# A two-layer hybrid attention trunk: copies and spills leave SP's queue, attention runs a few steps behind its projections

## The chip, the cores and the metric

The kernel runs on one core of a Trainium2 chip. A core has five engines that each run their own instruction stream in order: TensorE (PE) for matmuls, VectorE (DVE), ScalarE (ACT), GpSimd (POOL) and SyncE (SP), which in this kernel only issues DMA transfers. The metric is the device time of one execution in microseconds, lower is better. Matmul operands come from SBUF, results stand in PSUM, and weights, inputs and spilled tensors lie in HBM.

## The reference

Two layers, 512 tokens, width 1024, all float32. Each layer normalises its input, multiplies it by one wide matrix, runs two attention branches of the same input, gates them, projects them and adds the result to the input. Cut to its lines:

```python
h  = rms_norm(x, norm_w)
u  = h @ w_in                         # 1024 x 10240
qa, ka, va, za, qb, kb, vb, zb, ga, gb = split_cols(u)
qa, ka, qb, kb = partial_rope(...)    # first 16 of 64 channels of each head
ya = dilated_mixture(qa, ka, va) * silu(za)            # 16 heads of 64
ob = softmax(q1 k1) v - lam * softmax(q2 k2) v         # 8 heads, v of width 128
yb = rms_norm(ob, subln_w) * (1 - lam_init) * silu(zb)
merged = sigmoid(ga) * (ya @ w_proj_a) + sigmoid(gb) * (yb @ w_proj_b)
x  = x + merged @ w_out
...
return rms_norm(x, final_norm_w)
```

All attention is causal. `dilated_mixture` comes down to one softmax with a fixed additive bias that counts how many of three (window, dilation) patterns hold a pair of positions.

## The kernel before, in words

**Layout.** Activations stand transposed, channels on the 128 partitions and the 512 tokens in the free dimension. Each float32 operand is split into a rounded part and the rest (`split` for weights: `whi` by ACT at L102, `wlo` by DVE at L103), and each product is three matmuls: high by high, high by low, low by high (L264 to L266, L279 to L281).

**Weights.** `stream` lays the weights out as pieces of 512 KB in the order in which they are used. `load_to` issues a piece (`raw`, L96) on SP into a slot of the pool `blk`, `split` turns it into `whi` and `wlo` in a pool of three slots each. `blk` has 32 slots of 4 KB per partition, which nearly every large tile shares.

**Projections.** `proj_S` (gates and values v) works with seven products of sums of weight and activation blocks in place of eight; it has eight pieces, and POOL fetches the ones that are added (`T`, L112). `proj_T` (q/k of one unit, or one z tile) has two pieces and 48 matmuls of 512 columns, `proj_V` (`pa`, the projection of branch A) two pieces and 96 of 256 columns, `proj_W` (`pb` and `out`) four pieces.

**A layer.** First two z tiles, gate 0, v of branch A, gate 1, q/k of unit 0, v of branch B. Gates and v are spilled to HBM by SP (L442, L463). Then come 16 windows, one for each of 16 units: units 0 to 7 are pairs of heads of branch A, units 8 to 15 heads of branch B. Names carry (layer, branch, unit), so (0, 1, 6) is the seventh head of branch B in layer 0. Window w projects q/k of unit w+1, in some windows also a z tile or a quarter of `pa`, and beside them does the scores of unit w (`s_steps`, L477 to L508) and the values of unit w-1 (transposes `t` at L523, `o` at L555 and L613, in branch B also the norm `rms` with POOL's power at L224, `scale` at L636, the turn `ot` at L641, and `yf`, `yb`). `mix` orders the steps of the two units, and `run` spreads them evenly over the projection's steps of that window. After window 15, `pb` (with the values of unit 15 beside it), `out` and the next layer follow.

**q and k.** `ev_qk` takes the projection out of PSUM: DVE shuffle (L408) and product (L410), POOL product `sw` (L411), DVE sum (L412), ACT and DVE split (L418, L419) into `hl`, and then ten DMA copies by `move` (L403) that put the two halves of the partitions where the score matmuls want them: four of 64x512 into `qx`, and for each of two `kx` one of 64x1024 and two of 64x512. Scores of a unit start with the matmul L498 on `kx`.

**What sets the order.** The functions above emit instructions in a program order; then the tile framework's scheduler, with a timeline model of its own, orders each engine's stream. On the chip each stream runs in order, so an instruction that waits holds all behind it, DMA issues on SP's queue included.

Of the kernel before, what the change touches and what calls it, by code (L numbers as in the profile page):

```python
# [9 lines left out]
F32 = mybir.dt.float32  # L10
# [6 lines left out]
P = 128  # L17
# [15 lines left out]
def trunk_kernel(ctx: ExitStack, tc: tile.TileContext, x, xtok, ws, norm_w, subln_w, final_w, lams, negb, rope,  # L33
# [1 line left out]
    nc = tc.nc  # L35

    fix = ctx.enter_context(tc.tile_pool(name="fix", bufs=1))
    blk = ctx.enter_context(tc.tile_pool(name="blk", bufs=32))
    wpool = ctx.enter_context(tc.tile_pool(name="wpool", bufs=3))
    att = ctx.enter_context(tc.tile_pool(name="att", bufs=2))  # L40
    tmp = ctx.enter_context(tc.tile_pool(name="tmp", bufs=10))
# [46 lines left out]
    def load_to(i):  # L88
        while n_load[0] < min(i, len(loads)):
            j = n_load[0]  # L90
            if loads[j][0] == "add":
                n_load[0] += 1
                continue
            raw[j] = f4(f"raw{j}")
            to = raw[j].rearrange("p a t -> p (a t)")
            nc.sync.dma_start(to, ws[j])  # L96
            n_load[0] += 1

# [301 lines left out]
        return st_["h"][k]  # L400

    def move(to, of):
        nc.sync.dma_start(bits(to), bits(of))  # L403

    def ev_qk(key):
        def f(b, ps):
# [30 lines left out]
    def ev_v(layer, br):  # L437
        def f(tb, half, src):
            v = t2(f"v{layer}{br}{tb}{half}") if (tb >= 2 and half == 0) else src
            nc.scalar.activation(v, src, AF.Copy, scale=st_["rcol"][:, tb:tb + 1])  # L440
            to = v_dram[layer, br, 4 * half:4 * half + 4, :, tb].rearrange("u p c -> p u c")
            nc.sync.dma_start(to, v.rearrange("p (u c) -> p u c", u=4))  # L442
        return f

    def load_v(key, store):
# [13 lines left out]
    def ev_gate(layer, which):  # L459
        def f(tb, half, src):  # L460
            g = t2(f"g{layer}{which}{tb}{half}") if (tb >= 2 and half == 0) else src
            nc.scalar.activation(g, src, AF.Sigmoid, scale=st_["rcol"][:, tb:tb + 1])
            nc.sync.dma_start(g_dram[layer, which, tb, :, T * half:T * half + T], g)  # L463
        return f

    def ev_z(key):
# [8 lines left out]


    def s_steps(key, half, br, store):  # L477
        qx, kx = st_["qk"][key][0], st_["qk"][key][1 + half]
        mn = small.tile([P, 4], F32, tag="mn", name=f"mn{key}{half}")
        den = small.tile([P, 4], F32, tag="den", name=f"den{key}{half}")  # L480
        pr = store["p", half] = []
        store["den", half] = den

        def s(i):
            n = (i + 1) * P
            ps = pss.tile([P, T], F32, tag="s", name=f"s{key}{half}{i}")
            q = qx[:, half, i * P:(i + 1) * P]
# [19 lines left out]
            pr.append(p)  # L507
        return [(520, lambda i=i: s(i)) for i in range(4)]  # L508

    def t_steps(key, pr):  # L510
        def t(which):
            ps = pst.tile([P, T], F32, tag="t", name=f"t{key}{which}")
# [12 lines left out]
            nc.vector.tensor_tensor(dst[:, 1], ps[:, :n], bits(dst[:, 0]), OP.subtract)  # L525
        return [(440, lambda w=w: t(w)) for w in range(3)]
# [11 lines left out]
    def a_pair(layer, u):  # L538
# [34 lines left out]
        def scores(half):  # L573
            ss = s_steps(key, half, 0, store)
            if half == 0:
                load_v(key, store)
            else:
                ss = [(0, lambda: split_v(key, store))] + ss
            w, f = ss[-1]
            ss[-1] = (w, lambda: (f(), norm(half)))  # L580
            return ss

        def values(half):
            vv = t_steps((key, half), store["p", half]) + [(1200, lambda: pv(half))]
            return vv + [(0, fin)] if half else vv
        return scores, values

    def b_head(layer, u):
# [49 lines left out]
        def turn():  # L638
# [8 lines left out]
            nc.scalar.activation(y[:, 0], f, AF.Copy)  # L647
            nc.vector.tensor_tensor(y[:, 1], f, bits(y[:, 0]), OP.subtract)
            if u < 6:
                nc.sync.dma_start(yb_dram[layer, u], bits(y))  # L650

        def scores(half):
            ss = s_steps(key, half, 1, store)
            if half == 0:
                load_v(key, store)
            else:
                ss = [(0, lambda: split_v(key, store))] + ss
                w, f = ss[-1]
# [2 lines left out]

        def values(half):
            if half == 0:
                return t_steps((key, 0), store["p", 0]) + [(900, lambda: pv(0)), (900, lambda: pv(1))]
            return [(0, rms), (0, scale), (0, lambda: None), (430, turn)]
        return scores, values

    def back(layer):

        for u in range(6):  # L670
            y = st_["y"][layer, 1, u] = b4(f"yr{layer}{u}")
            nc.sync.dma_start(bits(y), yb_dram[layer, u])
# [27 lines left out]
    def gate(layer, which):  # L700
        return lambda: proj_S((layer, "gate", which), ev_gate(layer, which))

    pres = {}

    def pa(layer, i):

        c = slice(256 * i, 256 * i + 256)

        def pre():
            st_["pg", i] = f4(f"pg{layer}{i}").rearrange("p a (b c) -> p (a b) c", b=2)  # L710
            nc.sync.dma_start(st_["pg", i], g_dram[layer, 0, :, :, c].rearrange("t p c -> p t c"))

        def ev(tb, ps):
            t = st_["pg", i]
            nc.vector.tensor_tensor(t[:, tb], ps[:, :256], t[:, tb], OP.mult)
            if tb == 3:
                nc.sync.dma_start(pa_dram[layer, :, :, c].rearrange("t p c -> p t c"), t)
        pres[i] = pre
        return lambda: proj_V((layer, "pa", i), lambda k: st_["y"][layer, 0, k], ev)

    def turned(name, of):
# [35 lines left out]
    def outp(layer, i):  # L757
# [8 lines left out]

        def ev(tb, ps):
            nc.vector.tensor_tensor(r[tb], ps, r[tb], OP.add)
            nc.sync.dma_start(x1_dram[tb, :, i], r[tb])
            square(layer + 1, tb, i, r[tb])  # L770

        def turn(j):
# [91 lines left out]
    for layer in range(DEPTH):  # L864
# [64 lines left out]
def windows():  # L929
# [108 lines left out]
```

## Time and profile before

| | |
|---|---|
| runs | 1494.71, 1498.1 and 2704.91 us, median 1498.1 |
| profiled execution | 1494.3 us, its span 1492.5 us |
| mean granted TensorE clock | 0.967 of full speed |
| PE busy | 1389.8 us, 93% of the span |
| DVE, ACT, POOL busy | 1011.1 us (68%), 870.9 us (58%), 137.3 us (9%) |
| HBM traffic | 155.53 MB read, 31.46 MB written |

The profile shows one execution. Busy times are sums over a whole engine; PE's share is high everywhere, so what matters is where its idle time and its lower clock lie, and what ended each wait. In layer 0 the windows run from about 200 us to 650 us of the span, in layer 1 from about 950 us to 1400 us. Between and ahead of them lie the long projections.

### The profile page before, as it was taken

What the parts mean: (1) busy time and instruction counts of PE and PEld (TensorE: products, weight loads), DVE (VectorE), ACT (ScalarE), POOL (GpSimd) and SP (SyncE); (2) the same over time, 40 slices, a digit from 0 to 9 for tenths busy, and PEclk for the clock granted to TensorE, in tenths of its full rate; (3) what the DMA queues carried; (4) which work ended last, traced back from release to release, by engine and by line L of the source; (5) the groups of instructions that cost most, each with busy time, mean ns of one, the idle gap of its engine ahead of it and who ended that gap; (6) DMA issues with size and microseconds to landing.
All of it is one profiled execution on the core that took longest, in us unless ns stands there. A gap on an engine that the chain in (4) does not pass through costs nothing.

```text
span 1492.5 us, 19895 instructions
## 1 busy us (share of the span) xinstructions
PE 1389.8 (93%) x6856; PEld 1159.5 (78%) x6856; DVE 1011.1 (68%) x1959; ACT 870.9 (58%) x1655; POOL 137.3 (9%) x127
## 2 busy tenths in 40 slices
PE   7899999999989998889989999999999898997996
PEld 6788887877879787778878888878777786886785
DVE  6765667777777677635576667687777767767454
ACT  7866567776844645532367665668766545546232
POOL 2000001001010011000020000010111110010000
PEclk9999999999999999889999999999999999998998
DMA  9875634454365472962387746444444563729521
GB/s 340 221 192 144 195 103 119 122 169 114 106 163 170 148 207 76 298 258 71 132 203 189 208 100 184 127 113 114 141 131 128 157 186 97 233 78 335 193 71 57
DMA packets 108308, 238.63 MB, mean 160 GB/s; under 512 B 12464, under 2 KB 37168, under 8 KB 108208
## 3 DMA queue, kind: packets, MB, share of 16 engines
q1 hardware_dynamic: 103600, 220.58, 47.6%
q0 software_dynamic: 4608, 16.78, 6.5%
q8 instruction: 54, 0.88, 0.2%
q14 instruction: 46, 0.38, 0.1%
HBM read 155.53 MB, written 31.46 MB: 125 GB/s over the span
## 4 chain that ended last, share of the span: by engine, by line
PE 63%; DVE 10%; issue 9%; DMA 8%; ACT 6%; SPq 2%; POOL 0%; ACTq 0%; DVEq 0%; POOLq 0%
PE pj L264 8%; PE pj L265 8%; PE pj L266 8%; PE X L279 4%; PE X L280 4%; PE X L281 4%; DMA raw<-ws_d 3%; PE pw L279 2%; PE pw L280 2%; PE pw L281 2%; PE Y L281 2%; PE Y L280 2%; PE Y L279 2%; SPq L403 2%; ACT whi L102 1%
## 5 line engine op out<-in xcount | busy, mean ns | idle before, releaser
L103 DVE TENSOR_TENSOR wlo<-raw,whi 128x1024 fp32r<-128x1024 f32 x208 | 257.2, 1236 | 193.9 <-ACT whi L102 192.7
L102 ACT ACTIVATE whi<-raw 128x1024 fp32r<-128x1024 f32 x208 | 219.7, 1057 | 217.4 <-PE pw L281 77.4
L264 PE MATMUL pj<-h,whi 128*128 128x512 f32 x768 | 307.2, 403 | 15.2 <-DVE h L190 9.2
L265 PE MATMUL pj<-h,whi 128*128 128x512 f32 x768 | 304.9, 397 | 0.0
L266 PE MATMUL pj<-h,wlo 128*128 128x512 f32 x768 | 302.3, 395 | 0.0
L264 PEld LDWEIGHTS pj<-h,whi 128*128 128x128 f32 x768 | 145.8, 190 | 49.9 <-issue 9.2
L266 PEld LDWEIGHTS pj<-h,wlo 128*128 128x128 f32 x768 | 146.2, 190 | 29.5
L265 PEld LDWEIGHTS pj<-h,whi 128*128 128x128 f32 x768 | 146.3, 191 | 28.0 <-DVE h L191 0.4
L103 DVE TENSOR_TENSOR wlo<-T,whi 128x1024 fp32r<-128x1024 f32 x48 | 60.8, 1269 | 40.8 <-ACT whi L102 40.7
L102 ACT ACTIVATE whi<-T 128x1024 fp32r<-128x1024 f32 x48 | 50.6, 1055 | 18.3 <-PE Z L281 6.1
L280 PE MATMUL X<-wlo,h 128*128 128x512 f32 x128 | 51.2, 400 | 4.0 <-DVE wlo L103 4.0
L279 PE MATMUL X<-whi,h 128*128 128x512 f32 x128 | 48.2, 402 | 3.9 <-DVE z(1, 0, 0)_6927 L471 3.5
L279 PE MATMUL pw<-whi,mg 128*128 128x512 f32 x128 | 50.9, 400 | 0.0
L281 PE MATMUL X<-whi,h 128*128 128x512 f32 x128 | 50.9, 398 | 0.0
L280 PE MATMUL pw<-wlo,mg 128*128 128x512 f32 x128 | 49.9, 391 | 0.0
L280 PE MATMUL Y<-wlo,S 128*128 128x512 f32 x128 | 49.8, 389 | 0.0
L281 PE MATMUL Y<-whi,S 128*128 128x512 f32 x128 | 49.8, 389 | 0.0
L280 PE MATMUL X<-wlo,S 128*128 128x512 f32 x128 | 49.8, 389 | 0.0
L281 PE MATMUL X<-whi,S 128*128 128x512 f32 x128 | 49.8, 389 | 0.0
L281 PE MATMUL pw<-whi,mg 128*128 128x512 f32 x128 | 47.8, 393 | 0.0
L112 POOL DMA_DIRECT2D T<-ws_d x32 | 27.8, 870 | 200.3 <-ACT T L111 199.0
L279 PE MATMUL Y<-whi,S 128*128 128x512 f32 x128 | 44.9, 390 | 0.9 <-ACT whi L102 0.9
(3827 smaller groups left out, 3341.6 us busy)
## 6 DMA issues: line engine op xcount, KB each, us to landing
raw<-ws_d SPq DMA_DIRECT2D x192, 512.0 KB, 5.7
T<-ws_d POOLq DMA_DIRECT2D x32, 512.0 KB, 6.4
g_dram<-c SPq DMA_DIRECT2D x24, 256.0 KB, 2.2
v_dram<-c SPq DMA_DIRECT2D x24, 256.0 KB, 2.6
yr<-yb_dram SPq DMA_DIRECT2D x12, 512.0 KB, 8.8
pg<-g_dram SPq DMA_DIRECT2D x8, 512.0 KB, 4.3
pa_dram<-pg SPq DMA_DIRECT2D x8, 512.0 KB, 5.0
m<-g_dram SPq DMA_DIRECT2D x16, 256.0 KB, 7.5
```

The costliest lines, as they stand in the source:

```text
L102: nc.scalar.activation(whi[j], src, AF.Copy)
L103: nc.vector.tensor_tensor(wlo[j], src, bits(whi[j]), OP.subtract)
L112: nc.gpsimd.dma_start(out=flat(t), in_=add, accum_op=OP.add)
L264: nc.tensor.matmul(ps, w_h, hb[:, 0], start=(k == 0), stop=False)
L265: nc.tensor.matmul(ps, w_h, hb[:, 1], start=False, stop=False)
L266: nc.tensor.matmul(ps, w_l, hb[:, 0], start=False, stop=(k == 7))
L279: nc.tensor.matmul(ps, hh, w_h, start=first, stop=False, skip_group_check=True)
L280: nc.tensor.matmul(ps, hh, w_l, start=False, stop=False, skip_group_check=True)
L281: nc.tensor.matmul(ps, hl, w_h, start=False, stop=last, skip_group_check=True)
L403: nc.sync.dma_start(bits(to), bits(of))
```

## The change

Five edits. `move`, and the stores of `yb`, `pa` and `x1`, are issued by POOL in place of SP. The spills of gates and v are issued by ACT, which also computes them. SP keeps the loads. The weight pieces of `proj_T`, `proj_V` and `proj_W` get three slots of their own, and `blk` goes from 32 slots to 29; the pieces of `proj_S` stay in `blk`. The z tiles come behind q/k in their windows, and were ahead. And `run` for each window gives way to one `merge` over all 17 windows of a layer: a window's attention steps are placed by accumulated weights of the projection's steps, `LAG` = 6000 weights (about nine steps of `proj_T`) after the window's start and end. The 17th window is the values of the last head over the first 0.7 of `pb`'s first half. The functions `s_steps` and `t_steps` look up their tiles when a step runs, since steps now run later than the lists are made, and `load_v` is a step in the list.

```diff
+LAG = 6000
...
-    blk = ctx.enter_context(tc.tile_pool(name="blk", bufs=32))
+    blk = ctx.enter_context(tc.tile_pool(name="blk", bufs=29))
...
-            raw[j] = f4(f"raw{j}")
-            to = raw[j].rearrange("p a t -> p (a t)")
+            if loads[j][0] == "S":
+                t = f4(f"raw{j}")
+            else:
+                t = wpool.tile([P, 2, T], F32, tag="raw", name=f"raw{j}")
+            raw[j], to = t, flat(t)
             nc.sync.dma_start(to, ws[j])
...
     def move(to, of):
-        nc.sync.dma_start(bits(to), bits(of))
+        nc.gpsimd.dma_start(bits(to), bits(of))
...
-            nc.sync.dma_start(to, v.rearrange("p (u c) -> p u c", u=4))
+            nc.scalar.dma_start(to, v.rearrange("p (u c) -> p u c", u=4))
...
-            nc.sync.dma_start(g_dram[layer, which, tb, :, T * half:T * half + T], g)
+            nc.scalar.dma_start(g_dram[layer, which, tb, :, T * half:T * half + T], g)
...
-                nc.sync.dma_start(yb_dram[layer, u], bits(y))
+                nc.gpsimd.dma_start(yb_dram[layer, u], bits(y))
...
-                nc.sync.dma_start(pa_dram[layer, :, :, c].rearrange("t p c -> p t c"), t)
+                nc.gpsimd.dma_start(pa_dram[layer, :, :, c].rearrange("t p c -> p t c"), t)
...
-            nc.sync.dma_start(x1_dram[tb, :, i], r[tb])
+            nc.gpsimd.dma_start(x1_dram[tb, :, i], r[tb])
...
+    def merge(main, side):
+
+        done, j = 0.0, 0
+        for w, f in main:
+            f()
+            done += w
+            while j < len(side) and side[j][0] <= done:
+                side[j][1]()
+                j += 1
+        for _, f in side[j:]:
+            f()
...
-        for w, names in enumerate(WINDOWS):
-
-            side = []
-            for half in range(2):
-                here = heads[w][0](half)
-                side += mix(here, heads[w - 1][1](half)) if w else here
-            main = chain(*[todo[n[0]](layer, *n[1:]) for n in names])
-            main = [(0, pres[n[1]]) for n in names if n[0] == "pa"] + main
-            run(main + [(0, lambda: back(layer))] if w == 15 else main, side)
+
+        main, side = [], []
+        for w in range(17):
+            names = WINDOWS[w] if w < 16 else []
+            here = [heads[w][0](half) if w < 16 else [] for half in range(2)]
+            there = [heads[w - 1][1](half) if w else [] for half in range(2)]
+            steps = mix(here[0], there[0]) + mix(here[1], there[1])
+            new = [(0, pres_of(layer, n[1])) for n in names if n[0] == "pa"]
+            new += chain(*[todo[n[0]](layer, *n[1:]) for n in names])
+            if w == 15:
+                new.append((0, lambda: back(layer)))
+            if w == 16:
+                b = [pb(layer, i) for i in range(2)]
+                new = b[0][0]()
+            first, length = sum(m[0] for m in main), sum(m[0] for m in new)
+            end = first + length * (0.7 if w == 16 else 1) + LAG * (w < 15)
+            first += LAG * (w < 16)
+            side += [(first + (end - first) * (j + 1) / (len(steps) + 1), f) for j, (_, f) in enumerate(steps)]
+            main += new
+        merge(main, side)
...
-        w[at].insert(0, ("z", s // 4, s % 4))
+        w[at].append(("z", s // 4, s % 4))
```

Lines behind the edits are four to five higher in the changed kernel (`move` L403 is L407, `ot` L641 is L646), and about 17 higher from `merge` on. The scheduler orders each engine anew. SP issues 321 transfers where it issued 733, POOL 348 more than before, ACT 64 more; the matmuls and DVE's instructions are the same in number. Three places show the new order.

**SP around head (0, 1, 6) of layer 0.** `raw` is a weight piece, `vf` the reload of v, `pg` that of a gate. Before:

```order
L403 DMA qx(0, 1, 6)_5351<-hl(0, 1, 6)0_5348 64x512 x4
L96 DMA raw_5384<-ws_d 128x1024
L447 DMA vf(0, 1, 6)_5442<-v_dram 128x512
L650 DMA yb_dram<-yb(0, 1, 4)_5416 128x1024
L403 DMA kx(0, 1, 6)0_5432<-hl(0, 1, 6)1_5429 64x512
L403 DMA kx(0, 1, 6)0_5432<-hl(0, 1, 6)1_5429 64x1024
L403 DMA kx(0, 1, 6)0_5432<-hl(0, 1, 6)1_5429 64x512
L403 DMA kx(0, 1, 6)1_5436<-hl(0, 1, 6)1_5429 64x1024
L403 DMA kx(0, 1, 6)1_5436<-hl(0, 1, 6)1_5429 64x512 x2
L711 DMA pg_5446<-g_dram 128x4x256
L96 DMA raw_5452<-ws_d 128x1024
```

In the change:

```order
L100 DMA raw_5213<-ws_d 128x1024
L100 DMA raw_5270<-ws_d 128x1024
L100 DMA raw_5376<-ws_d 128x1024
L100 DMA raw_5410<-ws_d 128x1024
L451 DMA vf(0, 1, 5)_5204<-v_dram 128x512
L724 DMA pg_5404<-g_dram 128x4x256
L100 DMA raw_5506<-ws_d 128x1024
L100 DMA raw_5563<-ws_d 128x1024
L100 DMA raw_5730<-ws_d 128x1024
L451 DMA vf(0, 1, 6)_5497<-v_dram 128x512
```

The copies into `qx` and `kx` and the store of `yb` stood between the weight pieces; now only loads stand there.

**POOL around head (0, 1, 7).** `sw` is the rotary product of `ev_qk` (0 behind the bracket for q, 1 for k), `rs` the power of a head's norm. Before:

```order
L224 TENSOR_TENSOR rs(0, 1, 3)_4924<-rs(0, 1, 3)_4924,mhalf 128x4
L411 TENSOR_TENSOR sw(0, 1, 6)0_5342<-sw(0, 1, 6)0_5342,st 128x512
L224 TENSOR_TENSOR rs(0, 1, 4)_5251<-rs(0, 1, 4)_5251,mhalf 128x4
L411 TENSOR_TENSOR sw(0, 1, 6)1_5423<-sw(0, 1, 6)1_5423,st 128x512
L411 TENSOR_TENSOR sw(0, 1, 7)0_5505<-sw(0, 1, 7)0_5505,st 128x512
L411 TENSOR_TENSOR sw(0, 1, 7)1_5580<-sw(0, 1, 7)1_5580,st 128x512
L224 TENSOR_TENSOR rs(0, 1, 5)_5559<-rs(0, 1, 5)_5559,mhalf 128x4
L224 TENSOR_TENSOR rs(0, 1, 6)_5859<-rs(0, 1, 6)_5859,mhalf 128x4
L224 TENSOR_TENSOR rs(0, 1, 7)_6081<-rs(0, 1, 7)_6081,mhalf 128x4
```

In the change:

```order
L415 TENSOR_TENSOR sw(0, 1, 7)0_5462<-sw(0, 1, 7)0_5462,st 128x512
L407 DMA qx(0, 1, 7)_5471<-hl(0, 1, 7)0_5468 64x512 x4
L228 TENSOR_TENSOR rs(0, 1, 4)_5315<-rs(0, 1, 4)_5315,mhalf 128x4
L735 DMA pa_dram<-pg_5404 128x4x256
L415 TENSOR_TENSOR sw(0, 1, 7)1_5535<-sw(0, 1, 7)1_5535,st 128x512
L655 DMA yb_dram<-yb(0, 1, 4)_5483 128x1024
L407 DMA kx(0, 1, 7)0_5544<-hl(0, 1, 7)1_5541 64x512
L407 DMA kx(0, 1, 7)0_5544<-hl(0, 1, 7)1_5541 64x1024
L407 DMA kx(0, 1, 7)0_5544<-hl(0, 1, 7)1_5541 64x512
L407 DMA kx(0, 1, 7)1_5548<-hl(0, 1, 7)1_5541 64x1024
L407 DMA kx(0, 1, 7)1_5548<-hl(0, 1, 7)1_5541 64x512 x2
L228 TENSOR_TENSOR rs(0, 1, 5)_5628<-rs(0, 1, 5)_5628,mhalf 128x4
```

Between the two `sw` of a unit there are now the four copies into `qx`, an `rs` and a store; the six copies into `kx` come behind them.

**PE at the turn `ot` of a head of branch B.** `o` are its values, `pj` and `pv` projections, `s` scores, `t` transposes. Before, at head (0, 1, 2):

```order
L613 MATMUL o(0, 1, 2)1_4642<-vt(0, 1, 2)_4364,pt_103 128x256 x2
L265 MATMUL pj_1_4884<-h_7_190,whi_4745 128x512
L266 MATMUL pj_1_4884<-h_7_190,wlo_4746 128x512
L641 MATMUL ot(0, 1, 2)_4774<-ident,of(0, 1, 2)_4615 128x128 x4
L523 MATMUL t((0, 1, 3), 0)0_4826<-ident,p(0, 1, 3)0_4547 128x128
```

In the change, at the same head; the last of its `o` stands 76 rows above `ot`, and 68 of the rows between are `pv` matmuls:

```order
L284 MATMUL pv_3_5070<-wlo_4772,ya(0, 0, 0)_2097 128x256
L285 MATMUL pv_3_5070<-whi_4771,ya(0, 0, 0)_2097 128x256
L283 MATMUL pv_3_5070<-whi_4771,ya(0, 0, 1)_2322 128x256
L284 MATMUL pv_3_5070<-wlo_4772,ya(0, 0, 1)_2322 128x256
L646 MATMUL ot(0, 1, 2)_4841<-ident,of(0, 1, 2)_4679 128x128 x4
L528 MATMUL t((0, 1, 3), 0)0_4876<-ident,p(0, 1, 3)0_4596 128x128
```

In the change, at head (0, 1, 5), whose turn before had 14 rows of `pj` ahead of it and `o` farther up:

```order
L618 MATMUL o(0, 1, 5)1_5660<-vt(0, 1, 5)_5366,pt_103 128x256 x2
L507 MATMUL s(0, 1, 7)01_5851<-kx(0, 1, 7)0_5544,qx(0, 1, 7)_5471 128x256
L508 MATMUL s(0, 1, 7)01_5851<-kx(0, 1, 7)0_5544,qx(0, 1, 7)_5471 128x256
L507 MATMUL s(0, 1, 7)02_5871<-kx(0, 1, 7)0_5544,qx(0, 1, 7)_5471 128x384
L508 MATMUL s(0, 1, 7)02_5871<-kx(0, 1, 7)0_5544,qx(0, 1, 7)_5471 128x384
L646 MATMUL ot(0, 1, 5)_5806<-ident,of(0, 1, 5)_5627 128x128 x4
L528 MATMUL t((0, 1, 6), 0)0_5826<-ident,p(0, 1, 6)0_5524 128x128
```

The turn of (0, 1, 2) moved away from its `o`, that of (0, 1, 5) moved close to it.

## Rows read from the trace of the kernel before

**Rows 1.** The page: busy us of each engine, share of the span, instructions.

```profile
PE 1389.8 (93%) x6856; PEld 1159.5 (78%) x6856; DVE 1011.1 (68%) x1959; ACT 870.9 (58%) x1655; POOL 137.3 (9%) x127
```

**Rows 2.** Windows: stretch, length, busy us by engine, PEclk, DMA share, GB/s.

```profile
75.00:100.00 25.00, 24.90 (x111) 20.28 (x110) 14.98 (x13) 17.55 (x22) 3.45 (x4) 1.00 0.73 165
200.00:650.00 450.00, 414.00 (x2177) 349.12 (x2176) 326.40 (x760) 275.93 (x613) 45.64 (x37) 0.95 0.54 160
625.00:650.00 25.00, 17.55 (x67) 13.19 (x66) 17.35 (x49) 16.23 (x40) 1.01 (x1) 0.63 1.03 398
650.00:950.00 300.00, 295.27 (x1329) 242.55 (x1328) 181.63 (x214) 161.07 (x214) 22.36 (x23) 0.99 0.54 153
950.00:1400.00 450.00, 412.76 (x2179) 348.80 (x2178) 322.41 (x752) 272.24 (x611) 44.35 (x36) 0.95 0.55 163
```

**Rows 3.** PE's waits: who waits, for whom, us in total, times, longest.

```profile
PE ot(1, 1, 2)_11351 L641 <- DVE of(1, 1, 2)_11192 L636: 6.4, 1, 6.4
PE ot(0, 1, 2)_4774 L641 <- DVE of(0, 1, 2)_4615 L636: 6.0, 1, 6.0
PE ot(0, 1, 6)_5971 L641 <- DVE of(0, 1, 6)_5858 L636: 4.2, 1, 4.2
...
PE X L279 <- DVE z(1, 0, 0)_6927 L471: 3.5, 1, 3.5
...
PE ot(0, 1, 4)_5409 L641 <- DVE of(0, 1, 4)_5250 L636: 3.0, 1, 3.0
PE s(0, 0, 6)00_3104 L498 <- DMA kx(0, 0, 6)0_3080<-hl(0, 0, 6)1_3077: 2.8, 1, 2.8
...
PE t((1, 1, 6), 0)0_12377 L523 <- DVE p(1, 1, 6)0_12052 L603: 1.1, 3, 0.6
...
PE s(0, 0, 4)00_2588 L498 <- DMA kx(0, 0, 4)0_2564<-hl(0, 0, 4)1_2561: 1.0, 1, 1.0
```

**Rows 4.** SP's queue: waits of its DMA issues, in the same columns.

```profile
SPq L96 <- DVE wlo L103: 70.2, 18, 17.6
...
SPq L442 <- ACT c L440: 50.6, 23, 9.6
...
SPq L403 <- ACT hl(0, 1, 6)0_5348 L418: 20.1, 1, 20.1
```

**Rows 5.** The chain of waits around 515 us: start, length, what.

```profile
510.50 0.23 PE pj L266
510.73 0.12 PE o(0, 1, 2)0_4608 L613
...
514.02 0.53 ACT hl(0, 1, 4)0_4713 L418
...
514.57 0.47 SPq L403
...
515.73 4.54 DMA raw<-ws_d
...
520.37 1.06 ACT whi L102
...
522.85 1.02 POOL rs(0, 1, 2)_4616 L224
...
524.83 1.13 PE ot(0, 1, 2)_4774 L641 x4
```

**Rows 6.** Line L403: durations min, median, max in ns; landing of its copies.

```profile
L403 SPq DMA_DIRECT2D qx(0, 0, 3)_2162<-hl(0, 0, 3)0_2159 x4: 462/556/603, 262.6 to 264.4; - x4
...
DMA to landing us min/median/max: 2.2/3.3/9.3
```

**Rows 7.** Line L112: POOL's DMA issues, durations min, median, max in ns.

```profile
L112 POOL DMA_DIRECT2D T<-ws_d x32: 837/862/1052, 25.7 to 903.1; - x32
```

**Rows 8.** The page: DMA issues, KB each, median us from issue to landing.

```profile
raw<-ws_d SPq DMA_DIRECT2D x192, 512.0 KB, 5.7
T<-ws_d POOLq DMA_DIRECT2D x32, 512.0 KB, 6.4
```

More of the change, by code (lines that the diff above doesn't have):

```diff
@@ L477, in s_steps @@
     def s_steps(key, half, br, store):
[L478 to L482, printed above, removed]
-        def s(i):
+        def s(i):
+            if i == 0:
+                store["mn", half] = small.tile([P, 4], F32, tag="mn", name=f"mn{key}{half}")
+                store["den", half] = small.tile([P, 4], F32, tag="den", name=f"den{key}{half}")
+                store["p", half] = []
+            qx, kx = st_["qk"][key][0], st_["qk"][key][1 + half]
+            mn, den, pr = store["mn", half], store["den", half], store["p", half]
             n = (i + 1) * P
@@ L508, in s_steps, with t_steps @@
         return [(520, lambda i=i: s(i)) for i in range(4)]
-    def t_steps(key, pr):
+    def t_steps(key, store, half):
         def t(which):
+            pr = store["p", half]
             ps = pst.tile([P, T], F32, tag="t", name=f"t{key}{which}")
@@ L575, in scores @@
             if half == 0:
-                load_v(key, store)
+                ss = [(0, lambda: load_v(key, store))] + ss
             else:
@@ L583, in values @@
         def values(half):
-            vv = t_steps((key, half), store["p", half]) + [(1200, lambda: pv(half))]
+            vv = t_steps((key, half), store, half) + [(1200, lambda: pv(half))]
             return vv + [(0, fin)] if half else vv
@@ L654, in scores @@
             if half == 0:
-                load_v(key, store)
+                ss = [(0, lambda: load_v(key, store))] + ss
             else:
@@ L663, in values @@
             if half == 0:
-                return t_steps((key, 0), store["p", 0]) + [(900, lambda: pv(0)), (900, lambda: pv(1))]
+                return t_steps((key, 0), store, 0) + [(900, lambda: pv(0)), (900, lambda: pv(1))]
             return [(0, rms), (0, scale), (0, lambda: None), (430, turn)]
@@ L701, in gate, with pres_of, pre @@
         return lambda: proj_S((layer, "gate", which), ev_gate(layer, which))
-    pres = {}
+    def pres_of(layer, i):
+        def pre():
+            c = slice(256 * i, 256 * i + 256)
+            st_["pg", i] = f4(f"pg{layer}{i}").rearrange("p a (b c) -> p (a b) c", b=2)
+            nc.sync.dma_start(st_["pg", i], g_dram[layer, 0, :, :, c].rearrange("t p c -> p t c"))
+        return pre
     def pa(layer, i):
         c = slice(256 * i, 256 * i + 256)
-        def pre():
-            st_["pg", i] = f4(f"pg{layer}{i}").rearrange("p a (b c) -> p (a b) c", b=2)
-            nc.sync.dma_start(st_["pg", i], g_dram[layer, 0, :, :, c].rearrange("t p c -> p t c"))
         def ev(tb, ps):
@@ L716, in ev @@
             if tb == 3:
-                nc.sync.dma_start(pa_dram[layer, :, :, c].rearrange("t p c -> p t c"), t)
-        pres[i] = pre
+                nc.gpsimd.dma_start(pa_dram[layer, :, :, c].rearrange("t p c -> p t c"), t)
         return lambda: proj_V((layer, "pa", i), lambda k: st_["y"][layer, 0, k], ev)
@@ L890, in trunk_kernel @@
         todo = {"qk": qk, "z": zz, "pa": pa}
-        for w, names in enumerate(WINDOWS):
-            side = []
-            for half in range(2):
-                here = heads[w][0](half)
-                side += mix(here, heads[w - 1][1](half)) if w else here
-            main = chain(*[todo[n[0]](layer, *n[1:]) for n in names])
-            main = [(0, pres[n[1]]) for n in names if n[0] == "pa"] + main
-            run(main + [(0, lambda: back(layer))] if w == 15 else main, side)
+        main, side = [], []
[17 more added lines that the diff above has]
+        merge(main, side)
         last = layer + 1 == DEPTH
-        b = [pb(layer, i) for i in range(2)]
-        rest = heads[15][1](0) + heads[15][1](1) + [(0, lambda: None)] * 2
         if last:
@@ L905, in trunk_kernel @@
             nc.sync.dma_start(fwb, bass.AP(tensor=final_w.tensor, offset=final_w.offset, ap=[[0, P], [1, D]]))
-            run(b[0][0](), rest)
             run(b[1][0](), b[0][1]())
@@ L911, in trunk_kernel @@
             o = [outp(layer, i) for i in range(2)]
-            run(b[0][0](), rest)
             run(b[1][0](), b[0][1]())
```

## The prediction

> **What bounds the kernel now.** I read the page's first line, then the windows, then PE's waits, then the queues behind the longest waits. PE is busy for 93% of the span [rows 1], so nothing but PE's own lost time can be won. The windows show where that is: between 200 and 650 us PE idles 450 − 414.0 = 36.0 us and its granted clock is 0.95; between 950 and 1400 us it idles 37.2 us at 0.95; in the long projections from 650 to 950 us it idles 4.7 us at 0.99 [rows 2]. 0.95 is a mean over stretches at 2.4 GHz and at 1.2 GHz; it falls where PE has idled, most between 625 and 650 us, with 7.45 us idle and 0.63. In 450 us, 0.05 of the clock is 22.5 us. So each layer's windows lose 36 + 22.5 us, and one us of idleness goes with 0.62 us of lost clock.
>
> PE's waits name the idle time. Ten waits of the first score matmul for a copied `kx`, from 2.8 down to 1.0 us, make 17.9 us; six turns `ot` wait for their scaled `of`, 6.0, 3.0 and 4.2 us in layer 0 and within 0.4 us the same in layer 1, together 26.7 us [rows 3]. These two are 22.3 of a layer's 36 us. Both end in a late queue. SP's copy waits up to 20.1 us for `hl`, and weight loads stand behind it [rows 4]. The chain around 515 us shows what that does: ACT finishes `hl`, SP issues copies, only then the weight piece is loaded, 4.54 us, `whi` follows at 520.37, and behind it the power of the norm and at 524.83 the turn of head (0, 1, 2) [rows 5]. PE didn't wait for that weight; ACT and DVE did, in order, with the norm behind them.
>
> **The change, part by part**, per layer, in PE idle time.
>
> *kx.* The change gives `kx` more time: on PE's order, counting a 512-column matmul at 0.23 us and a 256-column one at 0.12 [rows 5], between 8 and 9 us lay between the last product that the slow copies rest on and their score matmul, where PE waited; now at least 12.7 us lie there for all units but the first (8.2). From 8 us of cover and 2.8 us of wait the copies' chain takes about 10.8 us. On POOL an issue costs 0.86 us [rows 7] where SP's cost 0.56 [rows 6]: for the three that the first score needs +0.9 us; landing costs +0.7 by the two rows of 512 KB [rows 8]. That is 12.4, under 12.7. All ten waits go: −9.0 (from 0 to −9).
>
> *Turns.* `ot` of heads 2 and 4 get 9 us between `o` and `ot` (68 matmuls of 0.12 us and four score matmuls at head 2): −6.0 − 3.0 = −9.0 in layer 0, −9.4 in layer 1, I take −9.2. Head 6 keeps its place and its 4.2 us. Head 5 now turns close behind its `o`, with four score matmuls of some 0.6 us between: 4.2 − 0.6 = **+3.6** (3.0 to 6.0, the other turns).
>
> *Late weights.* With only loads on SP, and three slots of their own, a piece can go out as soon as the one three before it is split. What of the other 13.7 us of idleness hangs on late pieces no row tells: between 0 and −13.7. I take −4.5, one load as long as that of [rows 5].
>
> *Lag and first units.* In four units of branch A the transposes now come closer behind their scores than before (from over 6 us of cover to between −2 and 4.5), so they may wait for DVE and ACT; before, waits of this kind had up to 1.1 us [rows 3]. Between 0 and 4.2 us each, as for a turn; near the small row: **+4** with the first `kx`.
>
> *Clusters.* The scheduler now puts attention work on PE in longer runs without a projection; the runs of over 3 us, added up from PE's order by the same matmul times, are 17.2 us in place of 6.4 in branch A and 11.1 in place of 7.9 at the end. There PE can wait for DVE's softmax. At worst all the added 14 us, at best none; DVE is busy 326.40 of 450 us [rows 2], so about a fifth of it, **+3**.
>
> *POOL.* 348 more issues of 0.86 us are 299 us beside its 137.3 [rows 1, 7], together 29% of the span: it isn't full. In 16 of 32 units the k product `sw` stands behind four copies, 3.4 us, and often a power, 1.02 us [rows 5]. The q half of the projection ends 24 matmuls of 0.23 us, 5.5 us, ahead of the k half, plus the attention in between, so most of it is over when `sw` could start: 0 (price without that cover below).
>
> *ACT's spills.* 64 issues at 0.46 to 0.87 us [rows 6, 7] are 29 to 56 us of ACT. In the long projections ACT is busy 17.55 of 25 us with PE full [rows 2]; a long projection of 168 matmuls of 0.23 us, 38 us, issues eight of them, 3.7 to 7 us. That fits: 0. SP loses its wait of 50.6 us for these values [rows 4]; what was behind it were loads that came in time.
>
> *Between the layers.* POOL's `T` loads and SP's pieces no longer stand behind the same stores; X's wait for `z`, 3.5 us [rows 3], goes: −3.5 once (0 to −3.5).
>
> *z behind q/k, slots in `blk`*: in the above by the order; 29 slots hold what 32 held with the pieces moved out: 0.
>
> The sum per layer is −9.0 − 9.2 + 3.6 − 4.5 + 4 + 3 = −12.1 us of idleness, times 1.62 with the clock −19.6; two layers −39.2, with −3.5 between them −42.7. Against the profiled execution's 1494.3 us that is **1452**. That execution lies 3.8 us under the median of the runs, 1498.1.
>
> **A page against the rows.** [Rows 4, 5] say that what moves is not the cost of issuing but loads held behind waiting copies. The Trainium skill ("DMA: Bandwidth & Descriptors", section "Issuing engines are not separate DMA queues") says that starting transfers from several engines saves only the sequencer's time, which it calls usually small. By that rule the queue terms would be nothing and the time the 1470 us of the first rival below; the chain of [rows 5] speaks against it, and no other row here decides it.
>
> **The rivals.**
>
> *The queues give nothing.* If loads come when they come because ACT and DVE split them late, the −4.5 goes, and −3.5 with it; order alone brings −7.6 × 1.62 × 2 = −24.6: **1470**. For it: PE itself has hardly a wait for a weight in the windows. Against: the chain of [rows 5].
>
> *Clusters give it back.* All 14 us in place of 3: +11 per layer, −1.1 × 1.62 × 2 − 3.5 = −7: **1487**. For it: DVE at 73% and PE's worst stretch, 625 to 650 us, is such a run. Against: less softmax is late when weights are early.
>
> *POOL holds the units* (slower). Its queue is in order, and DVE's sum L412 waits for `sw`, with all DVE work behind. If the 3.4 us of copies and the 1.02 us of power lie bare in 16 units, that is 4.4 × 16 = 71 us, with clock 115: 1452 + 115 = **1567**; with half of the units bare, **1509**; 1530 lies between. It decides where DVE reaches L412 of k before the copies of q are out, that is if `hl` of q is later than the 5.5 us. A further reason is that copies from POOL land later than 12.7 us.
>
> *ACT's spills stall the long projections.* 29 to 56 us in the open: 1481 to 1508, say **1493**. Against: 7 us of free time in 25.
>
> **How the numbers follow.** My forecast 0.47, the queues giving nothing 0.17, clusters 0.20, ACT 0.05, POOL 0.11. The range takes the forecast's own ends: without the prices of lag and clusters and with 3.0 at head 5, −9 − 9.2 − 4.5 + 3.0 = −19.7, times 1.62 times 2, with −3.5: 1427; upwards to the clusters' 1487. What is left out is POOL, part of ACT, and a low end in which late weights cost more than I took: 1427 to 1487. A difference of 2%, 30 us, is about what a measurement of this kernel tells from no change; against the median 1498.1 that is 1468. Faster: the forecast and the half of the first rival that lies under it, 0.47 + 0.09, and 0.04 of the clusters' case for a small price: 0.60. Slower by over 2%: most of POOL's, 0.10. Within: 0.30.
>
> **What would show it.** In the profile after: no wait of L502 (the score matmul, formerly L498) for `kx` over 1 us but the first unit's; no wait of `ot` of heads 2 and 4, one of about 3.6 us at head 5, 4 us at head 6; a granted clock of about 0.97 over the windows; PE idle about 24 us per layer there; SP without waits for `hl` or `yb`. POOL near 30% if its issue times count as busy. It would be wrong if DVE waits at L416 (formerly L412) for `sw` by several us in each of branch B's units, if the transposes of branch A's even units wait over 4 us each, or if ACT's `whi` in the long projections comes behind its DMA issues and PE waits there.

## The result, and the profile after

The changed kernel takes 1432.04 us (median of four, 1427.45 to 1436.93), the kernel before 1495.02 us (median of three, 1494.71 to 1498.1); the ratio is 0.9573 [0.9527, 0.9619]. A further execution of the kernel before took 2704.91 us, in a slow state, and is left out here, while the median of 1498.1 us in the prediction counts it. The forecast of 1452 us was 20 us too high, inside its range of 1427 to 1487 us. The profiled execution took 1436.93 us, its span is 1435.2 us; against this one, to which the prediction's sum belongs, the forecast was 15 us too high.

The page after, busy time, share of the span and instructions; it answers to [rows 1]:

```profile
PE 1364.9 (95%) x6856; PEld 1148.4 (80%) x6856; DVE 1010.7 (70%) x1959; ACT 873.7 (61%) x1655; POOL 325.9 (23%) x475
```

PE does the same matmuls in 24.9 us less busy time, and its mean granted clock over the span is 0.978 of full speed where it was 0.967. POOL is busy 23% of the span, not 29%: an issue there costs less than the prediction took.

Windows of the changed kernel; the columns are those of [rows 2]. All the windows of layer 0, then those of layer 1, then three stretches that still lose time:

```profile
200.00:650.00 450.00, 428.28 (x2301) 366.27 (x2300) 336.22 (x776) 281.80 (x625) 131.56 (x198) 0.97 0.59 165
...
920.00:1365.00 445.00, 424.45 (x2287) 362.59 (x2286) 334.91 (x773) 281.56 (x624) 131.52 (x198) 0.97 0.58 161
...
575.00:600.00 25.00, 16.58 (x86) 13.43 (x85) 17.07 (x48) 15.86 (x38) 5.43 (x9) 0.88 0.84 289
600.00:625.00 25.00, 19.06 (x79) 14.65 (x78) 12.46 (x34) 11.22 (x38) 1.62 (x2) 0.78 0.38 127
725.00:750.00 25.00, 18.90 (x78) 14.84 (x76) 21.43 (x28) 16.17 (x21) 7.16 (x6) 0.88 0.82 217
```

PE idles 21.7 and 20.5 us in the two stretches where it idled 36.0 and 37.2 [rows 2], and the granted clock went from 0.95 to 0.97. Two thirds of what is left of layer 0 is at the end of its windows: 14.4 us of the 21.7 lie between 575 and 625 us. The stretch from 725 to 750 us, where the next layer begins, idles 6.1 us.

PE's waits after, in the columns of [rows 3]:

```profile
PE X L283 <- DVE z(1, 0, 0)_6927 L475: 5.1, 1, 5.1
PE ot(1, 1, 6)_12548 L646 <- DVE of(1, 1, 6)_12460 L641: 4.9, 1, 4.9
...
PE ot(0, 1, 5)_5806 L646 <- DVE of(0, 1, 5)_5627 L641: 3.7, 1, 3.7
PE ot(1, 1, 5)_12383 L646 <- DVE of(1, 1, 5)_12204 L641: 3.3, 1, 3.3
PE s(0, 1, 7)02_5871 L507 <- DVE mn(0, 1, 7)0_5833 L509: 3.2, 1, 3.2
...
PE s(1, 0, 3)00_8939 L502 <- DMA kx(1, 0, 3)1_8762<-hl(1, 0, 3)1_8755: 2.8, 1, 2.8
...
PE s(0, 0, 3)00_2362 L502 <- DMA kx(0, 0, 3)1_2185<-hl(0, 0, 3)1_2178: 2.2, 1, 2.2
...
PE t((1, 1, 0), 0)0_10474 L528 <- DVE p(1, 1, 0)0_10257 L608: 0.3, 1, 0.3
```

Of ten waits for `kx` two are left, both in a unit that had none before. The turns of heads 2 and 4 wait no more; head 5 waits 3.7 and 3.3 us in their place, head 6 4.9. No transpose `t` waits over 0.3 us.

The copies of the changed kernel: one unit's issue times on POOL (min, median, max in ns), and the landing of all of them:

```profile
L407 POOL DMA_DIRECT2D qx(0, 0, 3)_2081<-hl(0, 0, 3)0_2078 x4: 516/526/537, 255.0 to 257.5; - x4
...
DMA to landing us min/median/max: 2.1/5.3/9.9
```

Against [rows 6] the issue costs the same on POOL as on SP, 0.53 against 0.56 us, and the copies land two us later.

### The profile page after: what moved, and what is told of

Read it like the earlier page. It is cut to its first block, busy times and chain, and to the rows that moved or that the text cites. A ratio compares the mean times of both kernels' runs of the same rounds, so it can differ in the third digit from the quotient of the medians.

```text
span 1435.2 us, 20086 instructions
## 1 busy us (share of the span) xinstructions
PE 1364.9 (95%) x6856; PEld 1148.4 (80%) x6856; DVE 1010.7 (70%) x1959; ACT 873.7 (61%) x1655; POOL 325.9 (23%) x475
## 4 chain that ended last, share of the span: by engine, by line
PE 85%; DVE 6%; ACT 3%; issue 3%; DMA 2%; POOL 1%; ACTq 0%; DVEq 0%; SPq 0%; POOLq 0%
PE pj L268 11%; PE pj L269 11%; PE pj L270 11%; PE pw L283 4%; PE pw L284 4%; PE X L283 4%; PE pw L285 4%; PE X L284 4%; PE X L285 4%; PE pv L285 2%; PE pv L284 2%; PE Y L284 2%; PE pv L283 2%; PE Y L285 2%; PE Y L283 2%
## 5 line engine op out<-in xcount | busy, mean ns | idle before, releaser
L107 DVE TENSOR_TENSOR wlo<-raw,whi 128x1024 fp32r<-128x1024 f32 x208 | 261.5, 1257 | 120.4 <-ACT whi L106 119.3
L268 PE MATMUL pj<-h,whi 128*128 128x512 f32 x768 | 303.1, 397 | 10.6 <-DVE h L194 8.7
L269 PE MATMUL pj<-h,whi 128*128 128x512 f32 x768 | 302.1, 394 | 0.0
L269 PEld LDWEIGHTS pj<-h,whi 128*128 128x128 f32 x768 | 145.3, 189 | 27.7 <-DVE h L195 0.4
```

Source lines behind the costliest of these rows:

```text
L107: nc.vector.tensor_tensor(wlo[j], src, bits(whi[j]), OP.subtract)
L268: nc.tensor.matmul(ps, w_h, hb[:, 0], start=(k == 0), stop=False)
L269: nc.tensor.matmul(ps, w_h, hb[:, 1], start=False, stop=False)
```

## The experiments

Each kernel is compared with the kernel before on the same chip. "Waits" is the sum over all rows of PE's waits in the profiled execution, for all kinds and then for the two of the prediction.

| kernel | median us | ratio [interval] | waits | `kx` | `ot` |
|---|---|---|---|---|---|
| before | 1495 to 1497 | | 89.5 | 17.9 | 26.7 |
| the change | 1432.0 | 0.9573 [0.9527, 0.9619] | 57.6 | 5.0 | 16.8 |
| copies back on SP | 1425.5 | 0.9533 [0.9510, 0.9556] | 53.9 | 0.2 | 16.3 |
| spills back on SP | 1427.3 | 0.9548 [0.9517, 0.9579] | 56.4 | 5.8 | 17.1 |
| lag 0 | 1450.1 | 0.9692 [0.9664, 0.9719] | 60.4 | 1.0 | 10.8 |
| order alone | 1440.5 | 0.9631 [0.9609, 0.9653] | 62.6 | 0 | 17.0 |
| queues alone | 1530.1 | 1.0237 [1.0201, 1.0274] | 107.4 | 29.7 | 24.5 |
| slots alone | 1497.8 | 1.0011 [0.9991, 1.0032] | 97.4 | 25.3 | 9.2 |
| queues and slots | 1495.4 | 0.9991 [0.9970, 1.0012] | 89.0 | 4.5 | 27.5 |
| `pa` late | 1447.9 | 0.9683 [0.9647, 0.9720] | 72.2 | 0.2 | 9.1 |
| z first | 1466.1 | 0.9791 [0.9762, 0.9821] | 76.0 | 13.2 | 17.3 |
| lag 0, z first | 1487.7 | 0.9925 [0.9896, 0.9953] | 82.0 | 3.5 | 24.0 |
| values late | 1423.9 | 0.9505 [0.9479, 0.9531] | 55.1 | 0.2 | 15.4 |
| order and slots | 1424.5 | 0.9526 [0.9497, 0.9556] | 53.1 | 0 | 15.8 |

**Copies back on SP.**

```diff
     def move(to, of):
-        nc.gpsimd.dma_start(bits(to), bits(of))
+        nc.sync.dma_start(bits(to), bits(of))
```

> The changed kernel with the copies into qx and kx back on SP; stores stay on POOL and spills on ACT. Theory Q (loads were held behind waiting copies): weight pieces come late again, ACT and DVE wait for them, turns and softmax behind them are late; 1450 to 1475 us against 1432. Theory O (order and cover did it, the issuing engine saves only its own time): 1425 to 1440 us.

1425.5 us: nothing is lost. Theory O holds here and theory Q falls: 320 copies can stand on SP among the loads at no cost. The copies now land in 3.9 us, and PE waits for `kx` 0.2 us in all.

**Spills back on SP.**

```diff
-            nc.scalar.dma_start(to, v.rearrange("p (u c) -> p u c", u=4))
+            nc.sync.dma_start(to, v.rearrange("p (u c) -> p u c", u=4))
...
-            nc.scalar.dma_start(g_dram[layer, which, tb, :, T * half:T * half + T], g)
+            nc.sync.dma_start(g_dram[layer, which, tb, :, T * half:T * half + T], g)
```

> The changed kernel with the spills of gates and v back on SP. The prediction put these at nothing, since the long projections had full PE before: 1427 to 1440 us. If pieces of the long projections or of the first windows were held behind the spills: over 1445 us, with PE's waits for weights between 40 and 220 us of the span.

1427.3 us, as the prediction had it: nothing.

**Lag 0.** In this kernel heads 2 and 4 of branch B use their gate tile before its Silu, since with z behind q/k and no lag the step stands behind them in program order. It leaves out a dependence that the change keeps, so its time may be shorter than with it.

```diff
-LAG = 6000
+LAG = 0
```

> The changed kernel with LAG = 0. Theory O: the first score matmul comes soon after its projection, the waits for kx come back with 1 to 3 us in ten units, and more at the turns; 1450 to 1470 us. Theory Q: the queues alone hold the gain; 1425 to 1440 us.

1450.1 us: 18 us are the lag's, at the low edge of what theory O wanted, and not for its reason. The waits for `kx` did not come back (1.0 us in all), those of the transposes are 10.2 us, where the change has 0.9, and 46 us of gain stay without a lag. PE's waits in all are only 2.8 us more than in the change, so most of the 18 us is not in the waits: PE is busy 9.6 us longer (first row under the next run), at a mean granted clock of 0.973, not 0.978. Why the clock falls more at lag 0 stays open.

**Order alone.** All the change's `gpsimd.dma_start` and `scalar.dma_start` lines are back on `sync`, and:

```diff
-    blk = ctx.enter_context(tc.tile_pool(name="blk", bufs=29))
+    blk = ctx.enter_context(tc.tile_pool(name="blk", bufs=32))
...
-            if loads[j][0] == "S":
+            if True:
```

> The changed kernel with every transfer back on SP and 32 shared slots for the weight pieces: only the new program order (lag, merge, z behind) is left. Theory O: 1430 to 1445 us. Theory Q: about 1470 us, the sum that the prediction gave to the order without the queues.

1440.5 us, as theory O had it: 55 of 63 us are the program order's, where the prediction gave it 25. The page of lag 0, then of this kernel:

```profile
PE 1374.5 (95%) x6856; PEld 1153.7 (80%) x6856; DVE 1009.6 (70%) x1959; ACT 870.7 (60%) x1655; POOL 327.3 (23%) x475
...
PE 1363.3 (95%) x6856; PEld 1146.5 (80%) x6856; DVE 1006.1 (70%) x1959; ACT 870.8 (61%) x1655; POOL 139.3 (10%) x127
```

With spans of 1448.6 and 1438.6 us, PE idles 74.1 and 75.3 us. The two differ by 10 us at nearly the same idle time.

**Queues alone.** The kernel before with the copies and stores on POOL and the spills on ACT.

```diff
-        nc.sync.dma_start(bits(to), bits(of))
+        nc.gpsimd.dma_start(bits(to), bits(of))
...
-            nc.sync.dma_start(to, v.rearrange("p (u c) -> p u c", u=4))
+            nc.scalar.dma_start(to, v.rearrange("p (u c) -> p u c", u=4))
...
```

> The kernel before with only the transfers moved: copies and stores on POOL, spills on ACT; old order, 32 shared slots. After the first four runs two routes seem to win nearly the same: the order alone 1440 us, and queues with slots at no lag 1450 us. Theory Q (queues): most of the second route is here, 1450 to 1465 us. Theory S (the three own slots are what lets pieces go early): 1480 to 1496 us.

1530.1 us: **slower** than before by 34 us, which neither theory had. The trace shows where. PE's waits of this kernel, eight for `kx` of up to 4.4 us, where before had ten of up to 2.8 [rows 3]:

```profile
PE s(1, 0, 4)00_9165 L498 <- DMA kx(1, 0, 4)0_9141<-hl(1, 0, 4)1_9138: 4.4, 1, 4.4
...
PE s(0, 0, 4)00_2588 L498 <- DMA kx(0, 0, 4)0_2564<-hl(0, 0, 4)1_2561: 4.1, 1, 4.1
```

The timeline of the same kernel around the second of them, POOL, SP and PE (start, length, instruction, idle time before and releaser):

```profile
313.29 0.54 POOL L403 DMA_DIRECT2D kx(0, 0, 4)0_2564<-hl(0, 0, 4)1_2561  x1 [6.42 <-ACT p(0, 0, 3)1_2440 L548]
314.10 1.05 POOL L403 DMA_DIRECT2D kx(0, 0, 4)0_2564<-hl(0, 0, 4)1_2561  x2 [0.27 <-DVE hl(0, 0, 4)1_2561 L419]
...
313.77 3.66 SPq L96 DMA_DIRECT2D raw<-ws_d  x4
...
322.36 0.55 PE L498 MATMUL s(0, 0, 4)00_2588<-kx(0, 0, 4)0_2564,qx(0, 0, 4)_2482 128*128 128x256 f32 x1 [4.09 <-DMA kx(0, 0, 4)0_2564<-hl(0, 0, 4)1_2561]
```

Just as POOL issues the copies, SP's queue sends four weight pieces, 2 MB, one behind the other. The last copy of `kx`'s first half is issued by 315.15, and the matmul can start at 322.36, 7.2 us later. The same unit with the three slots as well (below), in the same view:

```profile
303.86 0.54 POOL L406 DMA_DIRECT2D kx(0, 0, 4)0_2564<-hl(0, 0, 4)1_2561  x1 [4.63 <-ACT hl(0, 0, 4)1_2561 L421]
304.67 1.04 POOL L406 DMA_DIRECT2D kx(0, 0, 4)0_2564<-hl(0, 0, 4)1_2561  x2 [0.27 <-DVE hl(0, 0, 4)1_2561 L422]
...
296.14 7.09 SPq L99 DMA_DIRECT2D raw<-ws_d  x2
...
309.28 0.35 PE L501 MATMUL s(0, 0, 4)00_2588<-kx(0, 0, 4)0_2564,qx(0, 0, 4)_2482 128*128 128x256 f32 x1 [0.43 <-DMA kx(0, 0, 4)0_2564<-hl(0, 0, 4)1_2561]
```

There two pieces are issued between 296 and 303 us, ahead of the copies, none beside them, and the copies are there 3.6 us after the last issue. So queues that run apart can make transfers meet that one queue had kept in a row. That the burst of loads is what delays the copies is read from these two places and from the landing times (median 5.0 and at most 14.3 us with queues alone, 3.9 and 10.5 with slots); no run separates the burst from the rest.

**Slots alone.** The kernel before with the change's edit to `load_to` and `blk` of 29.

> The kernel before with only the three own slots for plain pieces and 29 shared ones; all transfers on SP, old order. Theory S: 1450 to 1470 us. Theory Q: pieces still stand behind waiting copies, 1485 to 1497 us.

1497.8 us: nothing, as theory Q had it. Waits move from `ot` (9.2 in place of 26.7 us) to `kx` (25.3 for 17.9), `pv` (15.3 for 6.2) and the transposes (15.0 for 3.1), and the sum does not fall.

**Queues and slots.** Both of these edits, old program order.

> The kernel before with both: transfers moved and own slots, old order. From the run at no lag, which nearly has the old order: 1445 to 1460 us. If that run's time came from z behind q/k and not from the transfers: over 1470 us.

1495.4 us: nothing again, the second case: the time of the run at lag 0 did not come from the transfers. This run decides on the late weights in the old order. In the kernel before, ACT waited for weight pieces; its row in the columns of [rows 3]:

```profile
ACT whi L102 <- DMA raw<-ws_d: 47.8, 34, 5.5
```

Here `whi` has no such wait at all. And yet the turns wait 27.5 us in all, as before: head 2's are shorter (4.4 us each, 6.0 and 6.4 before), head 4's longer (5.5 and 3.9 us, 3.0 before). Two of PE's rows of this kernel:

```profile
PE ot(0, 1, 4)_5409 L644 <- DVE of(0, 1, 4)_5250 L639: 5.5, 1, 5.5
...
PE ot(0, 1, 2)_4774 L644 <- DVE of(0, 1, 2)_4615 L639: 4.4, 1, 4.4
```

The chain around the turn of head (0, 1, 2) in this kernel shows why, in the columns of [rows 5]:

```profile
513.34 1.65 PE o(0, 1, 2)1_4642 L616 x14
...
517.82 0.48 DVE p(0, 1, 3)01_4569 L606
518.29 1.10 DVE p(0, 1, 3)0_4547 L606 x2
519.41 1.22 DVE wlo L106
520.79 1.95 POOL rs(0, 1, 2)_4616 L227
522.96 0.70 DVE of(0, 1, 2)_4615 L639
523.70 0.81 PE ot(0, 1, 2)_4774 L644 x4
```

From the last of `o` at 514.99 to the turn at 523.70 there are 8.7 us, nearly all of it DVE, ACT and POOL work in order, with the next head's softmax and a weight split in it, and no transfer. The late piece of [rows 5] was a link of that chain; without it the chain is still long enough for the turn to wait.

**`pa` late.** Copies on SP, and `pa` in windows 10, 12, 14, 15.

```diff
-    for i, at in enumerate((9, 10, 12, 14)):
+    for i, at in enumerate((10, 12, 14, 15)):
```

> The changed kernel with the copies on SP and the four quarters of pa in windows 10, 12, 14, 15 in place of 9, 10, 12, 14. If the end of the windows loses its time for want of projections beside the last heads' softmax, a quarter of pa there (96 matmuls of 0.12 us, 11 us) takes back about half of some 20 us per layer: 1400 to 1418 us. If that end is held by the chain from the last scores to the last turn however PE is filled: 1420 to 1430 us.

1447.9 us, worse than both expectations. The turns' waits fall to 9.1 us, but `pa` now waits itself:

```profile
PE pv L283 <- DVE pg L733: 20.1, 4, 6.3
...
PE ot(0, 1, 6)_5963 L646 <- DVE of(0, 1, 6)_5802 L641: 4.2, 1, 4.2
```

DVE takes `pa` out of PSUM at L733, where it multiplies it with the gate that SP loads back from HBM at L724. One of DVE's waits of this kernel, in the same columns:

```profile
DVE pg L733 <- DMA pg<-g_dram: 33.8, 8, 7.8
```

All eight quarters wait for that reload. The first is issued at 427.2 us and used at 432.5; with the copies on SP and `pa` in windows 9, 10, 12 and 14 it is issued at 404.6 and used at 420.4, and there DVE does not wait for it. So this run costs a late load, and does not tell whether the end of the windows lacks projections or is held by its own chain.

**z first, and lag 0 with z first.**

```diff
-        w[at].append(("z", s // 4, s % 4))
+        w[at].insert(0, ("z", s // 4, s % 4))
```

> The changed kernel with z ahead of q/k in its window again, lag 6000, queues and slots as changed. With queues and slots the old order took 1495 us, no lag with z behind 1450 us, the change 1432 us. Theory L (the lag is what gives): 1430 to 1445 us. Theory Z (z behind q/k gives, the lag only lets it be behind): 1475 to 1490 us.

> The changed kernel at lag 0 and with z ahead of q/k: of the new order only the single list of steps over all windows is left. Theories L and Z: 1485 to 1497 us, as with the old order. If the list itself gives (steps of a window no longer run out before its projections end): 1450 to 1465 us.

With the lag-0 run and the change these make a square, all with queues and slots moved:

| | z first | z behind q/k |
|---|---|---|
| lag 0 | 1487.7 | 1450.1 |
| lag 6000 | 1466.1 | 1432.0 |

Both edits give, and nearly add: z behind q/k 34 to 38 us, the lag 18 to 22 us. The larger figure for z and the smaller for the lag rest on the lag-0 kernel, which leaves out a dependence; 34 and 22 us do not. What else is new in the order (the single list with its 17th window) gives some 8 us against queues and slots in the old order (1495.4). Theories L and Z both missed the middle. In the run with z first and the lag, `kx` waits stand mostly in units whose q/k window has a z tile (the sixth window of branch A projects z, then q/k of unit 6), and `pa` waits, as above behind late reloads of the gate (DVE waits 13.2 us for them):

```profile
PE pv L283 <- DVE pg L733: 6.1, 3, 3.0
PE s(1, 1, 6)00_12100 L502 <- DMA kx(1, 1, 6)1_11975<-hl(1, 1, 6)1_11968: 5.2, 1, 5.2
...
PE s(0, 0, 6)00_3163 L502 <- DMA kx(0, 0, 6)0_3037<-hl(0, 0, 6)1_3034: 2.7, 1, 2.7
```

With z first and no lag the turns of heads 2, 4 and 6 wait as before the change, and those are the heads whose turn falls in a window with a z tile:

```profile
PE ot(0, 1, 6)_5971 L646 <- DVE of(0, 1, 6)_5859 L641: 4.4, 1, 4.4
...
PE ot(0, 1, 2)_4774 L646 <- DVE of(0, 1, 2)_4616 L641: 4.4, 1, 4.4
```

So the 48 matmuls of a z tile are work without a consumer in a hurry; ahead of q/k they delay it, behind q/k they cover its way through `ev_qk` and the copies. That is argued from which units wait; the times of the square are measured.

**Values late.** Copies on SP, and the values of head 6 in `pb`'s time, ahead of those of head 7.

```diff
+            if w == 15:
+                there6, there = there, [[], []]
             steps = mix(here[0], there[0]) + mix(here[1], there[1])
+            if w == 16:
+                steps = there6[0] + there6[1] + there[0] + there[1]
...
-            end = first + length * (0.7 if w == 16 else 1) + LAG * (w < 15)
+            end = first + length * (0.8 if w == 16 else 1) + LAG * (w < 15)
```

> The changed kernel with the copies on SP, and the values of head 6 moved out of window 15 into the first half of pb, ahead of those of head 7, up to 0.8 of it. At the windows' end the turn of head 6 and its second values wait some 5.6 us per layer; with pb's matmuls between, 5.6 x 1.62 x 2 = 18 us go: 1405 to 1413 us. If pb's own operands or the last head's turn then come late: 1420 to 1430 us.

1423.9 us, the second case, and no different from the copies back on SP (1425.5 us). The turn of head 6 is gone from the waits, that of head 7 has come in its place:

```profile
PE ot(1, 1, 7)_12744 L646 <- DVE of(1, 1, 7)_12684 L641: 4.1, 1, 4.1
PE ot(0, 1, 7)_6167 L646 <- DVE of(0, 1, 7)_6107 L641: 4.1, 1, 4.1
...
PE s(0, 1, 7)02_5852 L507 <- DVE mn(0, 1, 7)0_5829 L509: 3.3, 1, 3.3
```

**Order and slots.** Every transfer on SP, three slots as in the change.

> The changed kernel with every transfer on SP, as in the run of the order alone (1440 us), but with the three own slots. Theory: no moved queue gives anything, and what the change wins beyond its order comes from the slots, which let a piece go out ahead of the copies in program order: 1422 to 1430 us, as with the copies alone back on SP (1425.5). If stores on POOL or spills on ACT are what keeps pieces early: 1436 to 1444 us.

1424.5 us, as its theory had it. The new order and the slots, without one moved queue, make a kernel whose median is 7.5 us below the change's; the intervals of the two ratios, [0.9497, 0.9556] and [0.9527, 0.9619], overlap. Its windows in layer 0:

```profile
200.00:650.00 450.00, 431.39 (x2336) 369.56 (x2335) 338.11 (x780) 283.05 (x629) 46.80 (x38) 0.98 0.59 166
```

PE idles 18.6 us there, 3.1 less than in the change, and POOL is busy 46.80 us, not 131.56. With 32 shared slots the same order takes 1440.5 us: the slots, worth nothing in the old order, give 16 us in the new one. What waits in the order alone, and the second of its PE rows again in this kernel:

```profile
ACT whi L106 <- DMA raw<-ws_d: 32.6, 17, 4.2
...
PE s(1, 1, 7)00_12412 L502 <- DVE mn(1, 1, 6)1_12292 L509: 4.8, 1, 4.8
PE X L284 <- DVE wlo L107: 4.1, 1, 4.1
...
PE X L284 <- DVE wlo L107: 0.8, 1, 0.8
```

With the slots ACT's waits for pieces at `whi` are 1.8 us in place of 32.6, and the waits of score matmuls for DVE 10.1 us in place of 18.1. So in this order late pieces go together with time, as the prediction had it, though every load still stands among the copies on SP. That the 16 us come by this way is read from these sums; no run shows it alone.

## Why the prediction was right, and where not

**The bound** was right: what the change won is PE's idle time and the clock that goes with it. Idle time in the windows was forecast at 24 us per layer and is 21.7 and 20.5; the clock was forecast at 0.97 and is 0.97. In the profiled executions PE's idle time falls from 102.7 to 70.3 us and the span by 57.3 us, 1.77 for one, where the terms and the factor of 1.62 gave 27.7 and 42.7 us. That idle time has one price is an approximation: lag 0 and the order alone idle nearly the same and differ by 10 us, at granted clocks of 0.973 and 0.978.

**Which edit gives it** is where the prediction was furthest off. Its sum without the late weights and the gap between the layers, −7.6 us of idleness per layer or 24.6 us of time, was its price of the order alone (1470 us); the order alone gives 55 us. The rest of the account is the slots in the new order, 16 us, and the moved queues, which cost some 7 us in the medians.

**`kx` and the turns** came out near what was costed: the waits for `kx` fell from 17.9 to 5.0 us (−6.5 per layer, costed −9.0), those of heads 2 and 4 are gone, head 5's new wait is 3.7 and 3.3 us against 3.6. Order alone gives this, as the run of the order alone shows with no wait for `kx` and 17.0 us for turns.

**Late weights (−4.5)** have about the right size and the wrong carrier. −4.5 × 1.62 × 2 is 14.6 us, and the slots give 16 in the new order. But the loads need not have SP to themselves for it, which was the prediction's reason: with every transfer on SP the kernel takes 1424.5 us. And the price depends on the order: in the old one ACT's waits for pieces at `whi` can be taken away altogether with no change in time. That the term fits so well is in part luck, since it was set to the length of one load.

**Between the layers (−3.5)** the step failed: X's wait for z at the layer's start is 5.1 us, not gone. A neighbour that was not priced, X's wait for a split weight, fell from 4.0 to 0.5 us.

**POOL's copies** were mis-sized in two ways that nearly cancel in the sum: an issue costs 0.53 us and not 0.86, as the row of 128x1024 that the prediction took has another shape, and the landing grew by 2.0 us and not 0.7, 0.6 of it also with the copies on SP. The cost shows as two new waits for `kx`, 5.0 us in all, that go when the copies are on SP (0.2). The Trainium skill ("DMA: Bandwidth & Descriptors", section "Issuing engines are not separate DMA queues") says that issuing on more engines saves only the sequencer's time; the runs agree that nothing more is won, 1424.5 us with all transfers on SP against 1432.0 with them spread. They also show that spreading can cost: queues alone took 34 us more than the kernel before.

**Lag and first units (+4)** did not come: transposes wait 0.9 us in the whole kernel, 3.1 before. At lag 0 they wait 10.2 us, so the lag takes such waits away and does not bring them. Over two layers and with the prediction's factor the +4 is 13 us by which the forecast was too high; `kx`, which fell by 2.5 us per layer less than costed, takes 8 of them back. The waits of `pv` matmuls, which no term has, fell from 6.2 to 0.7 us.

**Clusters (+3)**: score matmuls waiting for DVE rose from 6.6 to 12.4 us, 2.9 per layer, as costed. About half of them, 3.2 us in each layer, stand at the windows' end with the turns of heads 5 and 6, where 14.4 us of layer 0's idle time now is.

**z behind q/k** was put at nothing of its own, inside the terms above. It is the largest edit, 34 to 38 us. The prediction read where PE's new order puts `kx` and the turns, and did not ask which edit put them there.

**The rivals.** "The queues give nothing" was right in what it says of the queues and 30 us too slow in its time, by the price of the order; its reason, that ACT and DVE split the loads late, was not tested. "POOL holds the units" did not come true in the change; but its last sentence, that copies from POOL land late, is how the waits for `kx` of the queues alone read. ACT's spills cost nothing, as forecast.

## What to carry to other kernels

A chain of waits that ends in a late load shows a link, not a cause: take the link away in one run before pricing it. Here it was worth nothing in the old order and 16 us in the new one. Put work that nobody waits for behind the work whose result takes a long way round, so that it covers the way. Transfers that are spread over queues can meet, as with the queues alone (1530.1 us); if they must move, first bound how many loads can be in flight, as three slots did.

## What the runs showed of the hardware

A copy of 64 rows costs POOL 0.53 us to issue and SP 0.56, so the row of 0.86 us for 128x1024 with an add was no guide. Copies issued by POOL landed in 5.3 us in the median in the change, 3.9 with the copies alone back on SP. That is not POOL's doing by itself: in the old order with the slots POOL's copies landed in 3.9 us too. The Trainium skill ("DMA: Bandwidth & Descriptors", section "SWDGE vs HWDGE vs iDMA") has GpSimd's and the other engines' transfers in different queues of each DMA engine, which takes turns between them; that fits copies that are slowed by a burst of loads from SP, and no run here shows the turns themselves.
